# Opening of a conditioned decoder trunk: modulation blocks ahead of weight tiles in the load queue, and constant tiles multiplied on TensorE between the first transposes

## The chip, the cores and the metric

The kernel runs on one core of a Trainium2 chip. A core has TensorE (PE in the profile; its weight loads are shown apart as PEld), VectorE (DVE), ScalarE (ACT), GpSimd (POOL) and SyncE (SP), and 16 DMA engines that they share. The metric is the device time of one execution in microseconds; before the change the median of three runs is 1215.93 us (1215.64 to 1216.92).

## The reference

One decoder layer on `x` of 1024 tokens by 1024 channels, all in 32-bit floats, conditioned by one vector `c`. Two mixers, HGRN2 and GLA, run on the same normalised input, both fed by one wide projection `w_in`; each branch is projected back, merged by sigmoid gates, and one output projection and a final norm follow. The change is in the part that makes the conditioned input and its first products:

```python
c_act = jax.nn.silu(c)
mod = c_act @ ada_w[l] + ada_b[l]
shift, scale, gate = jnp.split(mod, 3, axis=-1)
h = rms_norm(x, norm_w[l]) * (1.0 + scale[:, None, :]) + shift[:, None, :]
proj = h @ w_in[l]
```

`ada_w` is 1024 by 3072, so shift and scale alone need 8 MB of weights, for one row of result.

## The kernel before, in words

Everything is laid out with channels on the 128 partitions: `h` transposed is eight tiles of 128 channels (index `d`, 0 to 7) by 1024 tokens, worked on in two halves of 512 tokens. Matrix products keep 32-bit accuracy by splitting each operand into a high part in a reduced 32-bit format and the rest (`split`: a cast on ScalarE, L196, then a subtraction on VectorE, L197) and adding three products: high by high, high by low, low by high (`products(d, (0, 1, 2))`, six output tiles each, L352).

The opening, up to about 67 us, computes six columns of tiles (the GLA queries and two of its keys, `NG = 6`) for the first 512 tokens, while everything arrives from memory:

- The first four row tiles of `x` are loaded, squared (L203), scaled by their inverse root mean square (L210) and turned by TensorE transposes (`turn_x`, L219: four transposes per `d`, one per row tile); `copy_x` (L224) takes the result out of PSUM.
- Shift and scale come in five blocks, `blocks`, of one or two channel tiles each: d = 0; 1 and 2; 3 and 4; 5 and 6; 7. `load_mod` (L251) loads one: four loads of 256 KB for a block of one tile, eight for a block of two. Half of the sum over the input channels is accumulated on VectorE (`add_mod`, L265 and L267), the other half on TensorE (`mm_mod`, L277); `end_mod` adds the two (L283), reduces over partitions with a matmul by ones (L287) and leaves the factors `modv` and `amul` (L290, L292).
- `make_h(0, d)` applies them (L233) and splits the result.
- The raw weights come as eight tiles of 128 rows by 768 columns, 384 KB each (`load_wg`, L315); `prep_wg` splits each. Tiles 0, 1, 2, 5, 6 and 7 use three places in a fixed buffer in turn, so tile 5 needs tile 0 to be split, tile 6 tile 1 and tile 7 tile 2.

In this part the order of the instructions on TensorE, ScalarE and VectorE is the order in which the code writes them (`tc.manual_schedule`, until `order.close()`). An engine works its instructions in that order, so one that waits holds up all behind it. All these loads go through the SP queue, in order too. GpSimd stores finished pairs of `h` tiles (`store_h`, L238) as they come. After the opening a planner orders the instructions by its own costs, and the rest of the kernel follows: attention, further products, the branch and output projections.

The order of the opening is, in short: the loads of block 0, weight tiles 0, 1, 2, block 1, tiles 3 and 4, block 2; then the norm of `x`; `transpose_x(0, x_t, 0)`; block 0's modulation; `prep_wg(0)`; and a loop over the blocks that for each makes its `h` tiles, prepares the weight tiles of the next block, accumulates the next block on VectorE, and puts the products of this block on TensorE with the next block's `mm_mod` and `end_mod` between them.

Of the kernel before, what the change touches and what calls it, by code (L numbers as in the profile page):

```python
# [9 lines left out]
F32 = mybir.dt.float32  # L10
# [73 lines left out]
def hybrid_trunk_kernel(  # L84
# [6 lines left out]
    nc = tc.nc  # L91
# [99 lines left out]
    def split(src, hi=None, lo=None):  # L191

        if hi is None:
            hi = S.get(list(src.shape[1:]), F32R)
            lo = S.get(list(src.shape[1:]), F32R)
        nc.scalar.copy(hi, src)  # L196
        nc.vector.tensor_sub(lo, src, hi.bitcast(F32))  # L197
        return hi, lo
# [12 lines left out]

    turned = {}

    def turn_x(half, xs, d):
        if d % 2 == 0:
            hT[half, d // 2] = S.get([2, 512])
        turned[half, d] = mtile()
        for i in range(4):
            nc.tensor.transpose(turned[half, d][:, i * P:(i + 1) * P], xs[i][:, d * P:(d + 1) * P], ident)  # L219
        if d == KT - 1:  # L220
            S.free(*xs)

    def copy_x(half, d):
        nc.scalar.copy(hT[half, d // 2][:, d % 2, :], turned.pop((half, d)))  # L224

    def transpose_x(half, xs, d):
        turn_x(half, xs, d)
        copy_x(half, d)
# [14 lines left out]
    def load_mod(bi):  # L243
        d0, nd = blocks[bi]
        kq = 4 // nd
        mods[bi] = []
        for kk in range(KT // kq):
            b = S.get([kq, 2, nd * P])
            for half in range(2):
                c0 = half * D + d0 * P  # L250
                nc.sync.dma_start(b[:, :, half, :], ada_w[0, kk * kq * P:(kk + 1) * kq * P, c0:c0 + nd * P].rearrange(  # L251
                    "(k p) f -> p k f", p=P))
            mods[bi].append(b)
# [17 lines left out]
    def mm_mod(bi):  # L271
        kq = 4 // blocks[bi][1]
        w = 2 * blocks[bi][1] * P
        mod_ps[bi] = mtile()
        for j in range(4):
            k = 4 + j
            nc.tensor.matmul(mod_ps[bi][32 * j:32 * j + 32, 0:w], cs32[:, k, :],  # L277
                             mods[bi][k // kq][:, k % kq].rearrange("p a f -> p (a f)"), start=True, stop=True)
# [29 lines left out]
    raws = {}  # L308

    def load_wg(k):  # L310
        if k in (3, 4):
            raws[k] = S.get([T])
        else:
            raws[k] = xb_f[:, (k % 5 % 3) * 768:(k % 5 % 3) * 768 + 768]
        nc.sync.dma_start(raws[k][:, 0:NG * P], w_in[0, k * P:(k + 1) * P, C_GQ:C_GQ + NG * P])  # L315

    def prep_wg(k):
        raw = raws.pop(k)
        split(raw[:, 0:512], wa_hi[k // 2][:, k % 2, :], wa_lo[k // 2][:, k % 2, :])
        split(raw[:, 512:768], wb_hi[k // 4][:, k % 4, :], wb_lo[k // 4][:, k % 4, :])  # L320
        if k in (3, 4):
            S.free(raw)

    g_state = {}
    wga = cp.tile([P, KT, 16], F32, name="wga")
# [33 lines left out]

    load_mod(0)  # L360
    load_wg(0)
    load_wg(1)
    load_wg(2)
    load_mod(1)
    load_wg(3)
    load_wg(4)
    load_mod(2)
    for i in range(4):
        square_x(i, x_t[i])
        scale_x(i, x_t[i])  # L370
    vec_rows(rows_a, 24, R_SH)
    transpose_x(0, x_t, 0)
    add_mod(0)
    mm_mod(0)
    end_mod(0)
    prep_wg(0)
    x_t2 = []
    for bi, (d0, nd) in enumerate(blocks):
        ds = range(d0, d0 + nd)
        more = bi + 1 < len(blocks)  # L380
        nxt = range(blocks[bi + 1][0], sum(blocks[bi + 1])) if more else ()
        for d in ds:
            make_h(0, d)
            if (0, d + 2) in turned:
                copy_x(0, d + 2)
        if not more:
            break
        for d in nxt:
            prep_wg(d)
        add_mod(bi + 1)  # L390
        if nd == 1:
            for d in nxt:
                transpose_x(0, x_t, d)
            products(d0, (0,))
# [1324 lines left out]
```

## Time and profile before

| | us |
|---|---|
| median of three runs | 1215.93 |
| the profiled execution | 1216.46 |
| its span (first to last instruction) | 1214.8 |
| TensorE busy in the span | 1184.1 |
| VectorE busy | 790.9 |
| ScalarE busy | 546.9 |

The page's row of 40 slices gives the shape: TensorE is busy 5 tenths of the first slice of 30 us and 9 tenths or more of every other but the last. The DMA engines are busy 9 and 8 tenths of the first two slices; later they are less than half busy in most slices.

How to read it: times in the views are from the start of the span. In a timeline row stand the start, the length, engine, line and operation, what it writes and reads with its shape, and how many of a kind were merged; in brackets how long the engine was idle before, and what ended the wait. A matmul's length includes the time to run through the array, so that matmuls of a row overlap: the step from one start to the next tells the rate. The busy time of TensorE is a union of such stretches. A 32-bit matmul that is not split stands as two passes.

### The profile page before, as it was taken

To read this page: it belongs to the slowest core of one execution; us is meant where nothing else is said; L and a number is where in the kernel's file an instruction comes from. 1 tells how busy PE (TensorE), PEld (TensorE's weight loads), DVE (VectorE), ACT (ScalarE), POOL (GpSimd) and SP (SyncE) were. 2 spreads that over 40 slices of the span, in tenths; PEclk is the share of its full clock that TensorE was granted. 3 is DMA by queue.
4 is the path that set the end of the run, shared out by engine and by line. 5 is a ranking of instruction groups with operands and counts; after the bars stand their busy time and mean duration, and the time that the engine had idled before them with its cause. 6 is when DMAs were issued, how large, how long until landed. Compare 5 with 4: busy or idle time off the path is not lost.

```text
span 1214.8 us, 20860 instructions
## 1 busy us (share of the span) xinstructions
PE 1184.1 (97%) x8579; PEld 982.6 (81%) x8579; DVE 790.9 (65%) x1245; ACT 546.9 (45%) x797; POOL 123.8 (10%) x215
## 2 busy tenths in 40 slices
PE   5999999999999999999999999999999999999997
PEld 3777889889798888888887888877778888878886
DVE  4637444774848456877884365794653775988994
ACT  5646732434434244344332324455743544444554
POOL 4100000202111121121110101011220000000000
PEclk9999999999999999999999999999999999999999
DMA  9814000844444267255341112054697746435523
GB/s 320 277 70 139 18 19 19 293 141 161 156 152 149 66 207 249 94 179 169 108 174 47 59 53 70 36 174 158 227 343 277 260 160 208 135 104 173 174 104 122
DMA packets 130961, 183.51 MB, mean 151 GB/s; under 512 B 7467, under 2 KB 97633, under 8 KB 130866
## 3 DMA queue, kind: packets, MB, share of 16 engines
q1 hardware_dynamic: 117250, 136.87, 35.7%
q0 software_dynamic: 13568, 45.31, 9.6%
q8 instruction: 67, 1.10, 0.4%
q14 instruction: 28, 0.23, 0.1%
q10 hardware_dynamic: 48, 0.01, 0.0%
HBM read 132.87 MB, written 49.28 MB: 150 GB/s over the span
## 4 chain that ended last, share of the span: by engine, by line
PE 61%; issue 23%; DVE 3%; ACT 3%; POOL 2%; DMA 1%; POOLq 0%; ACTq 0%; DVEq 0%
PE pd L541 19%; PE pd L1343 9%; PE sc_ps L1343 5%; PE pm L1343 5%; PE pd L1520 3%; PE pd L643 2%; PE pd L644 2%; PE pd L645 2%; PE sc_ps L1520 2%; PE pm L848 1%; PE pd L352 1%; PE pm L829 1%; PE pm L850 1%; PE pm L1520 1%; PE sc_ps L352 1%
## 5 line engine op out<-in xcount | busy, mean ns | idle before, releaser
L541 PE MATMUL pd<-b,b 128*128 128x512 f32 x1632 | 387.4, 394 | 0.0
L541 PEld LDWEIGHTS pd<-b,b 128*128 128x128 f32 x1632 | 302.4, 188 | 64.8 <-issue 1.4
L1343 PE MATMUL pd<-b,b 128*128 128x512 f32 x720 | 173.7, 392 | 4.3 <-ACT b L1414 2.1
L1343 PEld LDWEIGHTS pd<-b,b 128*128 128x128 f32 x720 | 133.7, 188 | 35.7 <-ACT b L1414 3.2
L197 DVE TENSOR_TENSOR b<-b,b 128x1024 fp32r<-128x1024 f32 (+2 forms) x89 | 98.9, 1122 | 83.1 <-ACT b L196 65.4
L196 ACT CAST b<-b 128x1024 fp32r<-128x1024 f32 (+2 forms) x89 | 82.9, 948 | 92.1 <-DVE b L1199 14.6
L1286 DVE TENSOR_TENSOR b<-b,b 128x1024 fp32r<-128x1024 f32 x56 | 68.3, 1224 | 66.9 <-ACT b L1285 52.3
L1285 ACT CAST b<-b 128x1024 fp32r<-128x1024 f32 x56 | 58.3, 1050 | 73.9 <-PE pd L1343 20.6
L1343 PE MATMUL sc_ps<-b,b 128*128 128x512 f32 x324 | 79.4, 391 | 1.0 <-ACT scT L793 1.0
L600 PE MATMUL pd<-b,b 128*128 128x256 f32 x256 | 74.2, 290 | 0.0
L1264 DVE TENSOR_TENSOR b<-b,b 128x1024 fp32r<-128x1024 f32 x48 | 59.2, 1251 | 20.8 <-ACT b L1263 15.1
L602 PE MATMUL pd<-b,b 128*128 128x256 f32 x256 | 72.5, 283 | 0.0
L601 PE MATMUL pd<-b,b 128*128 128x256 f32 x256 | 72.4, 283 | 0.0
L1343 PEld LDWEIGHTS sc_ps<-b,b 128*128 128x128 f32 x324 | 60.3, 188 | 14.6 <-ACT scT L793 1.4
L1343 PE MATMUL pm<-b,b 128*128 128x512 f32 x300 | 72.1, 389 | 0.0
L1263 ACT CAST b<-b 128x1024 fp32r<-128x1024 f32 x48 | 49.9, 1050 | 41.2 <-PE pd L1343 16.0
L1343 PEld LDWEIGHTS pm<-b,b 128*128 128x128 f32 x300 | 56.3, 188 | 11.7
L352 PE MATMUL pd<-b,b 128*128 128x512 f32 x192 | 53.3, 410 | 2.0 <-ACT b L196 0.9
L1201 POOL DMA_DIRECT2D ws<-b x64 | 34.6, 541 | 192.0 <-DVE b L1195 86.5
L735 ACT COPY xb<-b 128x512 f32<-128x512 f32 x48 | 29.4, 620 | 49.4 <-PE sc_ps L715 26.7
L643 PE MATMUL pd<-b,b 128*128 128x512 f32 x128 | 51.3, 401 | 0.0
L644 PE MATMUL pd<-b,b 128*128 128x512 f32 x128 | 50.0, 390 | 0.0
(285 smaller groups left out, 1964.3 us busy)
## 6 DMA issues: line engine op xcount, KB each, us to landing
b<-in_w_in_dram SPq DMA_DIRECT2D x66, 512.0 KB, 4.2
ws<-b POOLq DMA_DIRECT2D x64, 256.0 KB, 3.3
b<-ws SPq DMA_DIRECT2D x32, 512.0 KB, 4.9
b<-in_x_dram SPq DMA_DIRECT2D x16, 512.0 KB, 5.7
b<-in_ada_w_dram SPq DMA_DIRECT2D x32, 256.0 KB, 6.9
b<-in_w_branch_dram SPq DMA_DIRECT2D x16, 512.0 KB, 4.4
b<-h SPq DMA_DIRECT2D x14, 512.0 KB, 4.3
wo<-b POOLq DMA_DIRECT2D x14, 512.0 KB, 5.7
```

Of the source, the lines that this page charges most:

```text
L196: nc.scalar.copy(hi, src)
L197: nc.vector.tensor_sub(lo, src, hi.bitcast(F32))
L352: nc.tensor.matmul(accs[f], wg(a, d, f), b[d][:, half * 512:half * 512 + 512], start=(d == 0 and n == 0), stop=(d == KT - 1 and n == 2))
L541: nc.tensor.matmul(ps[0:w, th * 512:(th + 1) * 512], a[:, k, 0:w], b[:, th * 512:(th + 1) * 512], start=(k == 0 and n == 0), stop=(k == KT ...
L600: nc.tensor.matmul(o, lh, hi[:, k % 4, :], start=(k == 0), stop=False)
L601: nc.tensor.matmul(o, lh, lo[:, k % 4, :], start=False, stop=False)
L602: nc.tensor.matmul(o, ll, hi[:, k % 4, :], start=False, stop=(k == KT - 1))
L643: nc.tensor.matmul(o, lh, hi[:, k % 2, :], start=(k == 0), stop=False)
L644: nc.tensor.matmul(o, lh, lo[:, k % 2, :], start=False, stop=False)
L1286: nc.vector.tensor_sub(lo, t, hi.bitcast(F32))
L1343: nc.tensor.matmul(o, a[:, sl], c, start=(p in (1, 5) and kt == 0 and n == 0), stop=(kt == 3 and n == 2), skip_group_check=True)
L1520: nc.tensor.matmul(o, a, b, start=(p in (1, 5) and kt == 0 and n == 0), stop=(kt == 3 and n == 2), skip_group_check=True)
```

## The change

What it does, in five parts:

1. In the SP queue the second modulation block goes ahead of weight tiles 1 and 2, and the third ahead of tiles 3 and 4.
2. `keep_busy(n)` multiplies two constant tiles, `ones` and `ident`, `n` times on TensorE into columns of `sc_ps` that the first products overwrite later. Six calls stand before the first transpose, 4, 8, 4 and 3 behind the four transposes of `d = 0`, one behind `mm_mod(0)` and two ahead of the first products. The results are not used.
3. The splitting of weight tiles 1 and 2 leaves its place ahead of the second block's accumulation. The casts of tile 1 go behind the first `end_mod` in the loop; the subtractions of tile 1, and tile 2 whole, go between `make_h(0, 1)` and `make_h(0, 2)`.
4. `prep_wg` becomes `prep_hi` (both casts) and `prep_lo` (both subtractions); the work is the same.
5. The loads of tiles 6 and 7 and of the last two modulation blocks are written behind that splitting, since they reuse its buffers. Tile 5 stays where it was.

```diff
+    def keep_busy(n):
+        for _ in range(n):
+            nc.tensor.matmul(sc_ps[:, 512:640], ones, ident, start=True, stop=True)
+
+    def turn_x(half, xs, d, gaps=(0, 0, 0, 0)):
...
             nc.tensor.transpose(turned[half, d][:, i * P:(i + 1) * P], xs[i][:, d * P:(d + 1) * P], ident)
+            keep_busy(gaps[i])
...
+    def wg_parts(k):
+        return ((raws[k][:, 0:512], wa_hi[k // 2][:, k % 2, :], wa_lo[k // 2][:, k % 2, :]),
+                (raws[k][:, 512:768], wb_hi[k // 4][:, k % 4, :], wb_lo[k // 4][:, k % 4, :]))
+
+    def prep_hi(k):
+        for raw, hi, _ in wg_parts(k):
+            nc.scalar.copy(hi, raw)
+
+    def prep_lo(k):
+        for raw, hi, lo in wg_parts(k):
+            nc.vector.tensor_sub(lo, raw, hi.bitcast(F32))
         raw = raws.pop(k)
...
     load_mod(0)
     load_wg(0)
+    load_mod(1)
     load_wg(1)
     load_wg(2)
-    load_mod(1)
+    load_mod(2)
     load_wg(3)
     load_wg(4)
-    load_mod(2)
...
-    transpose_x(0, x_t, 0)
+    keep_busy(6)
+    turn_x(0, x_t, 0, (4, 8, 4, 3))
+    copy_x(0, 0)
     add_mod(0)
     mm_mod(0)
+    keep_busy(1)
     end_mod(0)
...
+            if bi == 1 and d == 1:
+                prep_lo(1)
+                prep_wg(2)
+                load_wg(6)
+                load_mod(3)
+                load_wg(7)
+                load_mod(4)
...
-        for d in nxt:
-            prep_wg(d)
+        if bi:
+            for d in nxt:
+                prep_wg(d)
         add_mod(bi + 1)
         if nd == 1:
             for d in nxt:
                 transpose_x(0, x_t, d)
+            keep_busy(2)
             products(d0, (0,))
             mm_mod(bi + 1)
             products(d0, (1,))
             end_mod(bi + 1)
+            prep_hi(1)
             products(d0, (2,))
...
             load_wg(5)
-            load_wg(6)
-            load_mod(3)
-            load_wg(7)
-            load_mod(4)
```

More of the change, by code (lines that the diff above doesn't have):

```diff
@@ L212, in hybrid_trunk_kernel @@
     turned = {}
-    def turn_x(half, xs, d):
+    def keep_busy(n):
+        for _ in range(n):
+            nc.tensor.matmul(sc_ps[:, 512:640], ones, ident, start=True, stop=True)
+    def turn_x(half, xs, d, gaps=(0, 0, 0, 0)):
         if d % 2 == 0:
@@ L315, in load_wg, with prep_wg @@
         nc.sync.dma_start(raws[k][:, 0:NG * P], w_in[0, k * P:(k + 1) * P, C_GQ:C_GQ + NG * P])
-    def prep_wg(k):
+    def wg_parts(k):
[7 more added lines that the diff above has]
+            nc.vector.tensor_sub(lo, raw, hi.bitcast(F32))
         raw = raws.pop(k)
-        split(raw[:, 0:512], wa_hi[k // 2][:, k % 2, :], wa_lo[k // 2][:, k % 2, :])
-        split(raw[:, 512:768], wb_hi[k // 4][:, k % 4, :], wb_lo[k // 4][:, k % 4, :])
         if k in (3, 4):
             S.free(raw)
+    def prep_wg(k):
+        prep_hi(k)
+        prep_lo(k)
     g_state = {}
```

## The prediction

> **What bounds the kernel now.** I read the page's head first, then busy time by stretches, then the timeline of the first 40 us engine by engine (TensorE, VectorE and ScalarE, the SP queue), and last the issue-to-landing times of single loads.
>
> ```profile
> span 1214.8 us, 20860 instructions
> ```
>
> ```profile
> 14.00:22.00 8.00, 6.71 (x26) 4.47 (x26) 5.48 (x13) 5.19 (x11) 1.30 (x5) 1.00 1.08 362
> 22.00:26.00 4.00, 3.61 (x17) 1.59 (x16) 3.05 (x5) 0.00 (x0) 0.00 (x0) 1.00 1.07 369
> 26.00:38.00 12.00, 11.13 (x63) 8.10 (x62) 6.92 (x13) 5.60 (x10) 0.59 (x1) 1.00 1.08 367
> 38.00:67.00 29.00, 29.00 (x153) 22.94 (x153) 16.71 (x36) 18.89 (x35) 6.11 (x9) 1.00 0.61 209
> 74.00:110.00 36.00, 35.19 (x165) 26.63 (x164) 14.66 (x28) 20.73 (x28) 1.59 (x3) 1.00 0.41 135
> 110.00:800.00 690.00, 688.64 (x6122) 586.53 (x6121) 437.72 (x780) 273.87 (x401) 79.61 (x111) 1.00 0.37 119
> 800.00:900.00 100.00, 95.17 (x658) 76.56 (x657) 66.81 (x89) 58.72 (x84) 16.71 (x27) 1.00 0.64 223
> 900.00:1207.00 307.00, 306.40 (x1346) 251.43 (x1344) 227.16 (x260) 147.60 (x202) 4.27 (x8) 1.00 0.53 177
> ```
>
> The columns after the stretch are its length, then busy time of PE, PEld, DVE, ACT and POOL, the granted clock, the DMA share and GB/s. The reader is to see three things. TensorE has no idle time at all from 38 to 67 us, and 0.81 + 1.36 + 4.83 + 0.60 = 7.6 us of it from 74 us to its end: whatever the opening gains or loses by 38 us is carried to the end nearly one for one. Until 38 us the 16 DMA engines are full (share over 1) at 362 to 369 GB/s: the opening is a queue of loads with work hung on it. And the clock column says 1.00 even where, in the next rows, the same matmul takes nearly twice as long.
>
> ```profile
> 7.34 0.48 PE L219 MATMUL pm<-ident,b 128*128 128x128 f32 x1 [3.99 <-DVE b L210]
> 13.11 0.47 PE L219 MATMUL pm<-ident,b 128*128 128x128 f32 x1 [1.21 <-DVE b L210]
> 14.47 1.08 PE L277 MATMUL pm<-b,cs 128*32 128x256 f32 x8 [0.88 <-DVE scT L267]
> 17.02 1.95 PE L219 MATMUL pm<-ident,b 128*128 128x128 f32 x8
> 19.17 2.07 PE L352 MATMUL pd<-b,b 128*128 128x512 f32 x4 [0.20 <-ACT b L196]
> 21.04 1.05 PE L352 MATMUL sc_ps<-b,b 128*128 128x512 f32 x2
> 23.47 1.05 PE L277 MATMUL pm<-b,cs 128*32 128x512 f32 x4 [0.39 <-DMA b<-in_ada_w_dram]
> 24.45 1.21 PE L352 MATMUL pd<-b,b 128*128 128x512 f32 x4
> 25.50 0.62 PE L352 MATMUL sc_ps<-b,b 128*128 128x512 f32 x2
> 28.92 1.20 PE L352 MATMUL pd<-b,b 128*128 128x512 f32 x4
> 35.72 0.62 PE L352 MATMUL sc_ps<-b,b 128*128 128x512 f32 x2
> 37.13 1.02 PE L287 MATMUL pm<-ones,scT 128*128 128x1 f32 x8 [0.79 <-DVE scT L283]
> ```
>
> Two product matmuls take 1.05 us at 21.0 and 0.62 us at 25.5: TensorE runs at about half speed until some point between 21.5 and 24.5 us. The wait at 23.47 is for the last load of the second modulation block (mod1). The wait at 37.13 is the last one before the solid stretch: the third block's reduction (L287) waits for its accumulation on VectorE. That instruction is my clock: what it does, the kernel does.
>
> ```profile
> 27.40 0.82 ACT L233 ACTIVATE b<-b,modv,amul 128x512 f32<-128x512 f32 x1 [5.67 <-DVE amul L292]
> 30.21 2.28 ACT L196 CAST b<-b 128x512 fp32r<-128x512 f32 x5
> 30.86 2.57 DVE L197 TENSOR_TENSOR b<-b,b 128x512 fp32r<-128x512 f32 x5 [1.27 <-ACT b L196]
> 33.34 0.48 DVE L265 TENSOR_SCALAR scT<-b,cs 128x512 f32<-128x512 f32 x1
> 33.86 2.33 DVE L267 SCALAR_TENSOR_TENSOR scT<-b,cs,scT 128x512 f32<-128x512 f32 x3
> ```
>
> VectorE runs without a break from 30.86: the low part of h(2), the low parts of weight tiles 3 and 4 (five L197), then the accumulation (L265, three L267), one sum with TensorE's half of the block (L283), and at 37.13 the reduction. From the start of L265 to the reduction is 37.13 - 33.34 = 3.79 us.
>
> ```profile
> 8.24 3.11 SPq L315 DMA_DIRECT2D xb<-in_w_in_dram  x3
> 11.40 6.31 SPq L251 DMA_DIRECT2D b<-in_ada_w_dram  x8
> 18.10 1.09 SPq L315 DMA_DIRECT2D b<-in_w_in_dram  x2
> 19.60 6.14 SPq L251 DMA_DIRECT2D b<-in_ada_w_dram  x8
> 26.19 1.08 SPq L315 DMA_DIRECT2D xb<-in_w_in_dram  x2
> ```
>
> ```profile
> b<-in_ada_w_dram SPq DMA_DIRECT2D x32, 256.0 KB, 6.9
> xb<-in_w_in_dram SPq DMA_DIRECT2D x6, 384.0 KB, 6.2
> ...
> h<-b POOLq DMA_DIRECT2D x8, 512.0 KB, 3.1
> ```
>
> The first view is the SP queue in order of time, the second the size of one load of each kind (L251 loads modulation blocks, L315 weight tiles) and of the store of h.
>
> **The change, part by part.** *Loads.* Per queue order now: weight tiles 0 to 2 (x3), mod1 (x8), tiles 3 and 4 (x2), mod2 (x8), tiles 5 and 6. New: tile 0, mod1, tiles 1 and 2, mod2, tiles 3 and 4, tile 5. So mod1 passes two tiles of 384 KB, 786 KB at 367 GB/s = 2.1 us: complete at 23.4 - 2.1 = 21.3. Tiles 1 and 2 fall behind mod1, to 22.3 and 23.4. Tiles 3 and 4 fall behind mod2. The set of bytes up to tile 4 is what it was up to the end of mod2, so tile 4 lands when the last mod2 load lands now:
>
> ```profile
> L251 SPq DMA_DIRECT2D b<-in_ada_w_dram x1: 368/368/368, 25.4 to 25.4; - x1
> ...
> DMA to landing us min/median/max: 5.9/5.9/5.9
> ```
>
> 25.4 + 5.9 = 31.3 us, where today it is issued near 18.9, ahead of mod2.
>
> *Constant tiles.* 28 calls of keep_busy (6 + 19 + 1 + 2). A 32-bit matmul here is two passes (four L277 calls stand as x8 in the rows), and a half-speed pass of 128 columns costs what a transpose does: (1.95 - 0.42)/7 = 0.22 us, so 0.43 us a call, half that at full speed. The first six (2.6 us) lie in the idle 3.99 us before 7.34. The 19 between the four transposes are 8.2 us at half speed from 7.34 and so push the fourth transpose from 13.11 to about 14.7 and mm_mod(0) from 14.47 to 16.3, unless the clock rises in between. In before, full speed came 7 to 10 us after the first dense work (14.47); the same span from 7.34 gives 14.4 to 17.3. At 14.4, which I take because the whole stretch is dense, mm_mod(0) starts at 15.4, its eight passes (1.08 us) and the four of the reduction each take half, 0.5 us less, and products(0) start about where they do today, at 19.1; at 17.3 they start 1.3 us later. Both are covered by the next wait: six product matmuls take 1.5 us at full speed (24.45 to 25.50 for four), and mm_mod(1) cannot finish before mod1 is in at 21.3 (with 17.3 it loses 0.5 us, which the wait for tile 4 below takes up).
>
> *First to second block.* mm_mod(1)'s last passes go from 23.47 to 21.4, and what hangs on them in one chain (L283, reduction, amul, L233 at 27.40, casts) moves by as much, 2.0 us: L233 at 25.4, the products of d=1 at 26.9 instead of 28.92. VectorE's accumulation, now ahead of the low parts of tiles 1 and 2, is done in time (it starts near 18.9 and takes 0.48 + 2.33 us).
>
> *Second to third block, where it is lost.* Between h(1) and h(2) ACT now also has tile 2's two casts (0.9 us: five casts with two tiles take 2.28) and VectorE the low parts of tiles 1 and 2 (1.9 us: h(2)'s and two tiles' take 33.34 - 30.86 = 2.48, of which h(2) 0.6). h(2)'s low part thus starts at 30.86 - 2.0 + 0.9 = 29.7. Then VectorE, in order, must do tiles 3 and 4 before add_mod(2), and tile 4 is only in at 31.3: cast 0.62, both low parts 0.9, with hand-overs L265 at 32.9 instead of 33.34, so 0.44 us earlier. TensorE's work there took from 28.92 to 36.34 = 7.4 us, starts at 26.9 and is through at 34.3; it stands idle for some 2.7 us, where it stood 0.79. The gained 2 us become a wait for a weight tile.
>
> *Store of h.* The first one follows L233 of d=1, so it is issued 2 us earlier than now, at 26.5.
>
> ```profile
> L238 POOL DMA_DIRECT2D h<-b x1: 586/586/586, 28.5 to 28.5; - x1
> ...
> DMA to landing us min/median/max: 6.5/6.5/6.5
> ```
>
> Its 524 KB are 1.4 us of DMA. If they go ahead of tile 4, L265 is 1.4 us later; if behind, nothing. With the same 6.5 us it lands at 33.0, behind tile 4: I stay near the lower end and take 0.3.
>
> *Moved loads.* On SP, tile 6 and mod3 now stand behind VectorE's low part of tile 1 (28.3 us instead of 26.9). The queue then still holds tiles 3 to 5 and the store, work until some 33.5 us, so the engines do not run dry; uncovered, the whole later queue would slip by up to 1.4 us, and the block that uses mod3 comes a whole block of products later.
>
> *Sum.* -0.44 + 0.3 = about -0.2 us at the reduction, and with TensorE solid after it, at the end. The profiled execution took 1216.46 us (span 1214.8 plus 1.7 around it), 0.5 over the median 1215.93; the difference is applied to the median: **1215.7 us**. Its own bounds: tile 4 early after all, then VectorE's order binds (29.7 + 2.48 = 32.2, -1.2): 1214.7; store ahead of tile 4, -0.44 + 1.4: 1216.9.
>
> **Rivals.** 0.2% (2.4 us) is about what a measurement of this kernel can tell from no change.
>
> *A: the clock falls back in the new idle stretch.* For it: 2.7 us idle is longer than any the trace has at full speed. Against: after the longest there, 1.82 us, nine matmuls run at full speed.
>
> ```profile
> 892.87 2.34 PE L1343 MATMUL pd<-b,b 128*128 128x512 f32 x9 [1.82 <-ACT b L1414]
> ```
>
> Price: half speed for as long as in the opening, at least 7.1 us (14.47 to 21.5), loses 3.5 us of solid work: 1219.2, slower. It decides if the fall sets in anywhere between 1.82 and 2.7 us of idle time; chance 0.11. The Trainium skill ("TensorE: Matmul & The Clock Gate", section "HAM oscillation — how this bites in real kernels") lets the clock fall when an idle gap crosses a window of about 3.4 us; by that rule 2.7 us is safe, the sum stays at 1215.7 and A would get no chance, and the trace, whose gaps end at 1.82 us, neither shows nor denies it.
>
> *B: the constant tiles do not raise the clock.* For it: one operand is mostly zeros, and the eight transposes at 17.02, back to back, did not raise it. Against: these are ordinary matmuls. Then mm_mod(0) starts 1.8 us late and the one call behind it adds 0.2: products(0) start at 21.1, need 2.6 us at half speed, and mm_mod(1) comes at 23.7, 2.3 us after mod1; its passes, the next six products and the reduction add some 2 us at half speed; 0.6 us of slack before tile 4 and the sum's 0.2 come off. +3.5 us, 1219.4; chance 0.05. The Trainium skill ("TensorE: Matmul & The Clock Gate", section "Part 4: PE-mode transpose") says that transposes do not count as busy for the clock as matmuls do; the eight at 17.02 agree, and by that rule the constant tiles count, the sum stays and B would get no chance.
>
> *C: the order after the hand-written part changes.* There the planner orders by its own costs, and it sees other times. The 7.6 us of idle time after 74 us are single waits of up to 1.82 us; two such more or less are 3.6 us: 1219.5 or 1212.3. Since 4.83 of the 7.6 lie in one stretch, 800 to 900 us, a new order there has more to win than to lose: 0.15 for faster, 0.08 for slower.
>
> *D: the 2.0 us carry through.* That needs add_mod(2) ahead of tiles 3 and 4 on VectorE, or a load queue that runs otherwise than I read it; the first the order forbids. 1213.9, which is still within 0.2%; chance 0.05.
>
> **How the numbers follow.** Forecast 0.56 and D 0.05: within 0.2% 0.61. A 0.11, B 0.05, C 0.08: slower 0.24. C: faster 0.15. The predicted time is the forecast's. The range reaches down to 1213.0, which leaves out C's better part (0.12), and up to 1219.3, just past A, which leaves out about half of B and C (0.07).
>
> **What would show it.** Right: product matmuls near 19 us at 0.39 us each; mm_mod(1) ending near 22.4; L233 of d=1 near 25.4; VectorE waiting for a cast that waits for a weight load near 31; a PE wait of some 2.7 us before the third block's L287 near 37.0. Wrong: that L287 before 36 or after 38; 0.63 us matmuls behind it (A) or near 20 us (B); new waits after 74 us (C).

## The result, and the profile after

The changed kernel is slower: 1223.84 us median (1222.82 to 1225.49, 6 runs) against 1215.93 (1215.64 to 1217.28) on the same chip, a ratio of 1.0064 with a 95% interval of 1.0051 to 1.0077, so +7.9 us. The forecast was 1215.7, and its range ended at 1219.3. The profiled execution took 1223.68 us.

Below are the head of the page of the changed kernel and its stretches (length, then busy time of PE, PEld, DVE, ACT and POOL, granted clock, DMA share, GB/s).

```profile
span 1222.0 us, 20967 instructions
...
26.00:38.00 12.00, 9.14 (x42) 5.56 (x40) 7.73 (x14) 5.94 (x12) 0.59 (x1) 0.98 1.07 375
38.00:67.00 29.00, 27.82 (x135) 22.15 (x136) 17.07 (x37) 16.47 (x31) 6.11 (x9) 0.89 0.61 198
...
110.00:800.00 690.00, 686.57 (x6097) 583.47 (x6096) 434.27 (x775) 275.92 (x401) 77.64 (x109) 1.00 0.36 118
```

Three things differ from before. In 26 to 38 us TensorE is busy for 9.14 us instead of 11.13. From 38 to 67 us, which was solid, it is idle for 1.2 us (the end of a wait that began at 35 us), and its granted clock is 0.89 instead of 1.00. And from 110 to 800 us it has 3.4 us of idle time instead of 1.4, in a part of the kernel that the change does not touch.

The opening on TensorE, and what feeds it on ScalarE and VectorE (start, length, operation; in brackets the idle time before it and what ended it). L282, L292 and L369 are what L277, L287 and L352 were before; L328 and L332 split weight tiles; L270 and L272 are the accumulation; L223 are transposes.

```profile
11.59 0.27 PE L223 MATMUL pm<-ident,b 128*128 128x128 f32 x1
...
18.35 1.21 PE L369 MATMUL pd<-b,b 128*128 128x512 f32 x4 [0.63 <-ACT b L196]
...
21.49 1.05 PE L282 MATMUL pm<-b,cs 128*32 128x512 f32 x4 [0.39 <-DMA b<-in_ada_w_dram]
...
39.18 1.84 PE L292 MATMUL pm<-ones,scT 128*128 128x1 f32 x8 [3.95 <-DVE scT L288]
40.88 2.05 PE L369 MATMUL pd<-b,b 128*128 128x512 f32 x4
```

```profile
25.41 0.82 ACT L238 ACTIVATE b<-b,modv,amul 128x512 f32<-128x512 f32 x1 [2.10 <-DVE amul L297]
...
32.08 0.93 ACT L328 CAST b<-b 128x512 fp32r<-128x512 f32 x2 [2.41 <-DMA b<-in_w_in_dram]
33.80 0.93 ACT L328 CAST b<-b 128x512 fp32r<-128x512 f32 x2 [0.79 <-DMA b<-in_w_in_dram]
```

```profile
29.70 0.69 DVE L197 TENSOR_TENSOR b<-b,b 128x512 fp32r<-128x512 f32 x1 [0.22 <-ACT b L196]
...
35.40 0.48 DVE L270 TENSOR_SCALAR scT<-b,cs 128x512 f32<-128x512 f32 x1
```

Up to 30 us the prediction holds step by step. Then weight tile 4 lands at 33.8 us instead of 31.3, the accumulation starts at 35.40 instead of 32.9, TensorE stands idle for 3.95 us instead of 2.7, and behind it everything runs at half speed until about 43.5 us: the eight passes of the reduction take 1.84 us (1.02 before), the next four product passes 2.05 instead of 1.2. That is rival A. The later course can be followed on matching instructions. First three of the changed kernel, then two of the kernel before; two more of that stand in the prediction or in a later fence (892.87, 313.46):

```profile
112.95 0.50 PE L369 MATMUL pd<-b,b 128*128 128x512 f32 x1 [0.66 <-DVE b L348]
...
866.24 0.50 PE L1369 MATMUL pd<-b,b 128*128 128x512 f32 x1 [0.99 <-ACT b L1341]
...
899.89 0.50 PE L1369 MATMUL pd<-b,b 128*128 128x512 f32 x1 [1.74 <-ACT b L1440]
```

```profile
108.68 0.50 PE L352 MATMUL pd<-b,b 128*128 128x512 f32 x1 [0.81 <-DVE b L331]
...
859.83 0.50 PE L1343 MATMUL pd<-b,b 128*128 128x512 f32 x1 [0.15 <-ACT b L1315]
```

At 109 us the changed kernel is 4.3 us late: 2.05 from the late reduction (39.18 against 37.13), the rest from the slow clock. At 860 us it is 6.4 late and at 893 it is 7.0. So 2.7 us come from later waits, although every engine has the same instructions in the same order behind the opening. That was in no step of the prediction, and the experiments had to find it.

### The profile page after: what moved, and what is told of

Same layout as the page of the kernel before. It is cut to its first block, busy times and chain, and to the rows that moved or that the text cites. A ratio compares the mean times of both kernels' runs of the same rounds, so it can differ in the third digit from the quotient of the medians.

```text
span 1222.0 us, 20967 instructions
## 1 busy us (share of the span) xinstructions
PE 1193.7 (98%) x8635; PEld 991.2 (81%) x8635; DVE 790.4 (65%) x1245; ACT 547.4 (45%) x797; POOL 124.2 (10%) x215
## 4 chain that ended last, share of the span: by engine, by line
PE 62%; issue 22%; DVE 3%; ACT 3%; POOL 2%; DMA 1%; POOLq 0%; ACTq 0%; DVEq 0%
PE pd L567 20%; PE pd L1369 9%; PE sc_ps L1369 5%; PE pm L1369 5%; PE pd L1546 3%; PE pd L669 2%; PE pd L671 2%; PE pd L670 2%; PE sc_ps L1546 2%; PE pm L874 1%; PE pd L369 1%; PE pm L876 1%; PE pm L855 1%; PE pm L1546 1%; PE sc_ps L709 1%
## 5 line engine op out<-in xcount | busy, mean ns | idle before, releaser
L1369 PEld LDWEIGHTS pd<-b,b 128*128 128x128 f32 x720 | 133.6, 188 | 37.4 <-ACT b L1440 3.1
L197 DVE TENSOR_TENSOR b<-b,b 128x1024 fp32r<-128x1024 f32 (+1 forms) x85 | 97.2, 1151 | 86.3 <-ACT b L196 66.6
L196 ACT CAST b<-b 128x1024 fp32r<-128x1024 f32 (+1 forms) x85 | 81.3, 969 | 94.7 <-DMA b<-in_w_in_dram 14.5
L369 PE MATMUL pd<-b,b 128*128 128x512 f32 x192 | 53.6, 412 | 2.3 <-ACT b L196 1.3
```

What stands on the lines that cost most here:

```text
L369: nc.tensor.matmul(accs[f], wg(a, d, f), b[d][:, half * 512:half * 512 + 512], start=(d == 0 and n == 0), stop=(d == KT - 1 and n == 2))
L1369: nc.tensor.matmul(o, a[:, sl], c, start=(p in (1, 5) and kt == 0 and n == 0), stop=(kt == 3 and n == 2), skip_group_check=True)
```

## The experiments

Each kernel ran beside the kernel before on one chip. The table has the ratio to it with its 95% interval, and the difference worked out from the ratio at 1216 us. A profile is one execution, and runs of one kernel differ by 2 to 10 us, so a trace shows a mechanism and the ratio shows the size.

| kernel | ratio (95%) | us |
|---|---|---|
| changed kernel | 1.0064 (1.0051 to 1.0077) | +7.8 |
| the same, again (h4) | 1.0069 (1.0048 to 1.0091) | +8.4 |
| e1: without constant tiles | 1.0008 (0.9998 to 1.0019) | +1.0 |
| e2: constant tiles alone | 1.0040 (1.0027 to 1.0053) | +4.9 |
| e3: changed, accumulation first | 1.0019 (1.0008 to 1.0030) | +2.3 |
| e4: changed, wait filled | 1.0036 (1.0024 to 1.0048) | +4.4 |
| g1: length alone | 1.0019 (1.0010 to 1.0028) | +2.3 |
| g2: changed, whole packet | 1.0016 (1.0004 to 1.0027) | +1.9 |
| g3: e3, whole packet | 0.9986 (0.9977 to 0.9995) | -1.7 |
| g4: e3 without constant tiles | 0.9984 (0.9973 to 0.9994) | -1.9 |
| h1: e4, whole packet | 1.0014 (1.0005 to 1.0023) | +1.7 |
| h2: e2, whole packet | 1.0003 (0.9994 to 1.0012) | +0.4 |
| h3: e2, sum of head 7 on VectorE | 1.0033 (1.0019 to 1.0047) | +4.0 |
| k1: e2, sum of head 6 on VectorE | 1.0048 (1.0034 to 1.0061) | +5.8 |
| k2: meant to store h later | 1.0051 (1.0039 to 1.0064) | +6.2 |
| k3: g4, sum of head 6 on VectorE | 0.9996 (0.9985 to 1.0006) | -0.5 |

### Either part alone, and the two links of the chain

**e1**, load order and splitting without constant tiles:

```diff
-    keep_busy(6)
-    turn_x(0, x_t, 0, (4, 8, 4, 3))
-    copy_x(0, 0)
+    transpose_x(0, x_t, 0)
...
-    keep_busy(1)
...
-            keep_busy(2)
```

> The changed kernel without its constant tiles (no keep_busy); load order and splitting as changed. My theory: 56 fewer passes on TensorE put the packets that fetch instructions back to about 36 us, the third block's loads land in one go, tile 4 lands near 32.5 us instead of 33.8 (the early store of h still goes ahead of it), the third block's reduction (L292 of the changed kernel) comes near 38.0 instead of 39.2, TensorE's idle time before it falls under 3 us and the clock stays full behind it; TensorE at 45 us stands +0.5 to +1.5 us to the kernel before instead of +4.3; time 1216.5 to 1218.5. Rival 1, the order of loads alone does it: tile 4 at 33.8, idle 3 to 4 us, clock falls, +4 us at 45 us, time 1220 to 1224. Rival 2, without the tiles the clock rises 7 us later and the opening loses that in front: mm_mod(1) ends 2 us later than in the changed kernel (23.5 instead of 21.5).

**e2**, the kernel before with the 28 calls of `keep_busy` at their places and nothing else.

> The kernel before with the constant tiles alone (28 calls of keep_busy at the same places); loads and splitting as before. My theory: mm_mod(1) still waits for its load at 23.4 us, so the earlier clock wins nothing; the fetch of instructions comes near 26 us as in the changed kernel and holds up loads in flight by up to 1.2 us, so the third block's reduction (L287 of before at 37.1) comes at 37.1 to 38.3; time 1215.9 to 1217.5. Rival, the longer TensorE program shifts the fetches of the whole kernel and with them the waits after 220 us: +2.8 us behind the opening here too, time 1218 to 1220.

**e3**, the changed kernel with the third block's accumulation ahead of tiles 3 and 4 on VectorE:

```diff
-        if bi:
+        if bi > 1:
             for d in nxt:
                 prep_wg(d)
         add_mod(bi + 1)
+        if bi == 1:
+            prep_wg(3)
+            prep_hi(4)
...
             end_mod(bi + 1)
+            if bi == 1:
+                prep_lo(4)
```

> The changed kernel with the third block's accumulation (add_mod(2)) ahead of weight tiles 3 and 4 on VectorE, and tile 4's low part behind end_mod(2). My theory: the reduction no longer waits for tile 4; it comes at 35.2 to 35.8 us when TensorE is through with its products, instead of 39.2, TensorE stands idle there under 1 us and the clock stays full: at 45 us TensorE is 1.5 to 2 us ahead of the kernel before, 6 us ahead of the changed one; time 1214 if nothing is added behind the opening, 1217 if the 2.8 us there come all the same. Rival, tile 4 is not what the block waits for (its own late load is, or the products of d=3 then wait for tile 3 and 4 just as long): a wait of 2 us or more remains between 35 and 42 us, time 1219 or more.

**e4**, the wait filled with products that nobody reads:

```diff
         pm = mtile()
+        if bi == 2:
+            for _ in range(14):
+                nc.tensor.matmul(pm[:, 256:384], ones, ident, start=True, stop=True)
```

> The changed kernel with 14 more constant products (28 passes, 3.1 us at full clock) on TensorE ahead of the third block's reduction, into columns of its own accumulator that nobody reads: the wait for tile 4 stays, the idle time goes. My theory: the reduction still comes at 39.2 us, but its passes and the products behind it run at 0.39 us for two passes instead of 1.05: TensorE at 45 us stands +2.0 us to the kernel before instead of +4.3; time 1221.5, 2.3 under the changed kernel. Rival, the clock does not fall through idleness (something else holds it, such as the loads): half-rate products between 39 and 43 us all the same, time 1223.8.

The reduction of the third block on TensorE's timeline, in e1, then in e3 and e4:

```profile
36.97 1.02 PE L287 MATMUL pm<-ones,scT 128*128 128x1 f32 x8 [1.60 <-DVE scT L283]
```

```profile
34.73 1.04 PE L292 MATMUL pm<-ones,scT 128*128 128x1 f32 x8 [0.45 <-ACT b L229]
```

```profile
34.17 3.29 PE L292 MATMUL pm<-ident,ones 128*128 128x128 f32 x28
37.33 1.05 PE L295 MATMUL pm<-ones,scT 128*128 128x1 f32 x8
```

e1 has the reduction at 36.97, where the prediction had 37.0 and e1's own expectation 38.0, a clock that holds, and a time that cannot be told from before. Its wait is only 1.60 us, because without the tiles TensorE's own work ends later (35.4 us instead of 34.4 in g2 below), so e1 does not test what a wait of 2.7 us does. The new load order alone neither wins nor loses. e3 shows that tile 4 is what the block waits for: with the accumulation ahead of it the reduction comes at 34.73, 2.4 us ahead of before. In e4 the clock holds; but its tile 4 was early too, so this run does not price the fall by itself.

The misses are in the totals. e2 should have cost nothing and costs 4.9 us, with an opening that is not late. e3 is 2.4 us ahead in the opening and ends 2.3 us behind. The constant tiles cost some 4 us far from where they stand.

### Why the tiles cost: the packets that carry instructions

The page's DMA part has queues of their own for instructions. The larger one stands alike in both kernels (a second, q14, has 28 packets and 0.23 MB in both):

```profile
q8 instruction: 67, 1.10, 0.4%
```

67 packets, 1.10 MB: 16 KB each. TensorE has 2 x 8635 matmul and load instructions in the changed kernel, 258 to a packet. The 28 calls add 112 instructions, so every later packet comes nearly half a packet earlier: in e2 at 27, 48, 70 and 101 us, in the kernel before at 35, 59, 80 and 112. Here are the DMA queues of the changed kernel in 24 to 28 us, and of the kernel before in 34 to 38 us, where its first packet is (packets, MB, share of 16 engines):

```profile
q1 hardware_dynamic: 1355, 1.40, 107.9%
q8 instruction: 1, 0.02, 1.7%
```

```profile
q1 hardware_dynamic: 1421, 1.37, 103.5%
q8 instruction: 1, 0.02, 1.8%
```

1.7% of 16 engines over 4 us is 1.1 us of one engine. In 24 to 28 us the queue of loads is full and carries the third block and tiles 3 and 4. That the packet holds up the part of a load that shares its engine is an inference: no view here shows the engines one by one.

To test this, tiny products were added: as many instructions as the tiles have, or as many more as make up one packet of 256.

```diff
+    def pad(n):
+        for i in range(n):
+            nc.tensor.matmul(sc_ps[32 * (i % 4):32 * (i % 4) + 32, 512:513], ident[:, 0:32], one_t,
+                             start=True, stop=True)
...
     vec_rows(rows_a, 24, R_SH)
+    pad(28)
```

**g1** is the kernel before with `pad(28)`; **g2** the changed kernel with `pad(36)`; **g3** is e3 with `pad(36)`; **h2** is e2 with `pad(36)`. **g4** is e3 without constant tiles and without `pad`.

> The kernel before with 28 tiny products (128x32 by 128x1, one column each) on TensorE behind the transpose of rows_a, in its idle time before 7.34 us; nothing else. They lengthen TensorE's program by as many instructions as the constant tiles (28 calls, 112 instructions) but are too short to change the clock or the opening. My theory now: TensorE's instructions come in packets of 16384 bytes, one per about 256 instructions, each a single packet on one DMA engine that holds up the loads of that moment by about 1 us; 112 instructions more move every later packet 8 to 13 us ahead of the work, as in the run with the tiles alone (first one near 27 us instead of 35, one at 299 us in the burst of loads of 291 to 302 instead of 287), and with them the waits at 253 to 315, 812 and 860 us. Expected: the opening within 0.3 us of the kernel before at 45 us, packets as in the tiles-alone run, time 1219 to 1221.5. Rival: the cost of the tiles is their work or the earlier clock, not the length: time 1216 to 1217, packets unmoved.

> The changed kernel with 36 tiny products more (128x32 by 128x1) ahead of its constant tiles: 64 calls, 256 instructions, one packet of instructions in whole, so that all packets behind the opening fall where they fall in the kernel before. My theory: packets near 35, 59, 80, 111 us as in the kernel before; tile 4 lands at 31.2 to 32.0 us instead of 33.8, the third block's reduction comes at 36.7 to 37.7 us instead of 39.2, the idle time ahead of it is under 2.7 us; behind the opening no more than 1 us is added; time 1216 to 1218, as without the tiles. Rival 1, length is not it: 1221 to 1224. Rival 2, a packet that now falls into 5 to 15 us delays the loads of the opening: L282 of the first block later than 15 us, and 1 us of that stays.

> The kernel with the third block's accumulation ahead of weight tiles 3 and 4 (constant tiles and new load order kept), with the same 36 tiny products more, a whole packet of instructions in all. My theory: the opening is 2.4 us ahead of the kernel before at 37 us as in that kernel's own run, and now stays so: no 2.4 us wait at 812 us and no fall of the clock behind it; time 1213.5 to 1215, under both kernels. Rival, the 4.7 us that kernel lost behind the opening come from its being early, not from the packets: time 1217.5 to 1219.

> The kernel with the third block's accumulation ahead of weight tiles 3 and 4, without any constant tiles: new load order, program length as before. My theory: the clock rises near 21 us as in the run without tiles, the reduction no longer waits for tile 4 and comes at 34.8 to 35.6 us (before 37.1, with tiles 34.7); packets as in the kernel before; time 1214 to 1215.5. Rival, without the tiles the slow clock until 21 us is now on the path: reduction at 36 us or later, time 1216 or more; or the early opening itself breeds the later waits: 1217.5 to 1219.

> The kernel with the constant tiles alone (old load order), with 36 tiny products more, 256 instructions in all. My theory: its 4.4 us over the kernel before come from packets of instructions moved by 112 instructions, and go: packets near 35, 59, 80, 287 us again, waits at 314 and 863 us back under 0.7 and gone, time 1215.5 to 1217.5. Rival: the tiles cost by the earlier clock or their work, whatever the length: 1219.5 to 1222.

36 more products on TensorE make three kernels faster: the changed kernel goes from +7.8 to +1.9, e3 from +2.3 to -1.7, e2 from +4.9 to +0.4. And length alone, with an opening like that of before, costs 2.3 us (1.2 to 3.4). So the cost hangs on where the packets fall, and not on the work of the tiles. How the packets turn into lost time can be followed at one place in the trace. In 291 to 303 us a burst of loads ends with a block that VectorE waits for; it feeds the totals for which TensorE waits near 314 us. The queues and the row of VectorE in e2, then in g1:

```profile
q8 instruction: 1, 0.02, 0.6%
...
302.61 0.69 DVE L1204 TENSOR_TENSOR b<-b 128x512 f32<-128x512 f32 x1 [1.71 <-DMA b<-in_w_in_dram]
...
314.10 0.89 PE L724 MATMUL sc_ps<-xb,b 128*32 128x48 f32 x64 [1.40 <-DVE tot L727]
```

```profile
q8 instruction: 1, 0.02, 0.6%
...
303.04 0.69 DVE L1201 TENSOR_TENSOR b<-b 128x512 f32<-128x512 f32 x1 [1.62 <-DMA b<-in_w_in_dram]
...
314.52 0.89 PE L721 MATMUL sc_ps<-xb,b 128*32 128x48 f32 x64 [1.30 <-DVE tot L724]
```

The same rows of the kernel before and of h2, where no instruction packet falls into this stretch:

```profile
301.72 0.69 DVE L1195 TENSOR_TENSOR b<-b 128x512 f32<-128x512 f32 x1 [0.71 <-DMA b<-in_w_in_dram]
...
313.46 0.89 PE L715 MATMUL sc_ps<-xb,b 128*32 128x48 f32 x64 [0.66 <-DVE tot L718]
```

```profile
301.18 0.69 DVE L1210 TENSOR_TENSOR b<-b 128x512 f32<-128x512 f32 x1 [0.64 <-DMA b<-in_w_in_dram]
...
312.73 0.89 PE L730 MATMUL sc_ps<-xb,b 128*32 128x48 f32 x64 [0.40 <-DVE tot L733]
```

With a packet in the burst the block is in 0.9 to 1.9 us later and TensorE waits 1.3 to 1.4 us instead of 0.4 to 0.7. The Trainium skill ("Runtime: NRT & Kernel Launch", section "Instruction fetch mechanics") says that instructions come in 16 KiB blocks of 256 and that crossing a boundary costs little and is mostly hidden. The size agrees. It is hidden from TensorE in so far as no wait of it here ends on an instruction; it is not hidden from the loads.

The traces of the other kernels agree. Behind the opening TensorE works the same instructions in the same order in all of them, so that its delay against the kernel before can be read instruction by instruction. At this place, between 308 and 318 us, the delay grows by 0.6 to 1.0 us in all nine kernels whose packets are shifted (the changed kernel, h4, e2, e3, e4, g1, h3, k1, k2) and shrinks by 0.1 to 0.4 us in the seven others. From 862 to 895 us it grows by 0.4 to 1.3 us in eight of the nine (not in e4) and in none of the seven. A third loss, 0.5 to 1.4 us near 255 us, stands in all nine, but about 1 us of it also in e1, g3 and k3, so that the packets are not its only cause.

What length alone costs (2.3) is less than what a whole packet takes away (4.0 to 5.9). The profiled executions show where the rest lies. e2 and e3 lose 2.5 us near 813 us, by a wait with a fall of the clock behind it that g1 does not have (its cause is below). At 45 us the changed kernel is 1.6 us later than g2, because tile 4 comes late. Whether the shift brings about the loss near 813 us is not shown.

Constant tiles without the shift win nothing: g2 and e1 cannot be told apart, nor g3 and g4. **g4 has the lowest ratio, 1.9 us under before** (0.7 to 3.3), with no constant tiles at all. Its reduction:

```profile
35.03 1.04 PE L287 MATMUL pm<-ones,scT 128*128 128x1 f32 x8 [0.47 <-ACT b L224]
```

### Why the clock falls

g2 is the changed kernel with the packets where they were. ScalarE's casts of tile 4, VectorE's accumulation and TensorE's reduction in it, and its stretches:

```profile
31.39 0.93 ACT L333 CAST b<-b 128x512 fp32r<-128x512 f32 x2 [0.16 <-DMA b<-in_w_in_dram]
```

```profile
33.00 0.48 DVE L275 TENSOR_SCALAR scT<-b,cs 128x512 f32<-128x512 f32 x1
```

```profile
36.78 1.67 PE L297 MATMUL pm<-ones,scT 128*128 128x1 f32 x8 [2.42 <-DVE scT L293]
38.31 2.05 PE L374 MATMUL pd<-b,b 128*128 128x512 f32 x4
```

```profile
36.00:40.00 4.00, 3.22 (x12) 2.96 (x13) 0.96 (x3) 1.08 (x2) 0.00 (x1) 0.62 1.09 355
40.00:44.00 4.00, 4.00 (x11) 3.09 (x11) 2.95 (x6) 3.34 (x7) 0.54 (x1) 0.53 1.15 324
...
647.60:651.40 3.80, 3.80 (x11) 2.97 (x11) 1.23 (x1) 0.69 (x2) 0.00 (x0) 0.55 0.30 79
```

Tile 4 (31.4), accumulation (33.0) and reduction (36.8) are the forecast's 31.3, 32.9 and 37.0. The idle time is 2.42 us where 2.7 were forecast, and it is enough: the clock falls, and at 44 us TensorE is 2.9 us behind before, from 0.35 ahead.

**h1** fills that wait as e4 did, with `pad(22)` so that all calls together make a whole packet.

> The changed kernel with a whole packet of instructions in all (22 tiny products ahead of the constant tiles) and with 14 more constant products ahead of the third block's reduction, which fill the wait for tile 4 that was 2.42 us idle in the run with the whole packet alone. My theory: the clock no longer falls behind the reduction (it cost 2.8 us there), so TensorE at 45 us is within 0.6 us of the kernel before, against +2.6 to +2.8 in the run with the whole packet; time 1216 to 1217.5, 2 to 3 under that run's. Rival, the fall has another cause than the idle time: half-rate products behind 37 us and 1219 to 1220 as there.

```profile
38.18 0.95 PE L300 MATMUL pm<-ones,scT 128*128 128x1 f32 x8
```

The clock holds, although the reduction comes later than in g2, and at 109 us TensorE stands at +0.6 us instead of +2.6: the mechanism is as expected. The total is not: +1.7 against +1.9, where 2 to 3 us less were expected; 2 us is at the edge of what the two intervals allow, so the run does not bear the price out. This execution lost 1.6 us again near 648 us, by a fall of the clock such as g2 has at 647.6 (the row above). It follows four short products of norms that take 4.1 us (two passes each start about 1 us apart), without idle time. The kernel before has the same four and a clock of 1.00 behind them in its profiled execution; of all 17 profiled executions four show this fall (g2, h1, h4 and k1). So the clock falls in some executions and not in others, without a wait. In how many of the runs behind the ratios of g2 and h1 the clock fell, at 37 us or here, is not known.

### The changed kernel again, and three edits that settled less

**h4** is the changed kernel once more.

> The changed kernel once more, unchanged, beside the others on the same chip. My theory: tile 4 lands at 31.5 to 34 us, by which DMA engine the packet of instructions near 25 us hits (the run with the clock kept had 32.0 with the same packet), so the wait before the third block's reduction is 2.0 to 4.0 us, always long enough for the clock to fall; time 1220.5 to 1224. Rival: the 33.8 us is the rule: wait 3.9 us and 1223 to 1225 again.

```profile
39.17 1.06 PE L292 MATMUL pm<-ones,scT 128*128 128x1 f32 x8 [3.81 <-DVE scT L288]
40.10 2.06 PE L369 MATMUL pd<-b,b 128*128 128x512 f32 x4
```

Tile 4 came at 33.8 us again and the time is 1224.15 us, so the rival of this expectation holds. The clock falls again, here behind the reduction: the products take 2.06 us. **k2** was to store h later (`for i in (1, 0, 2, 3)` in `store_h`):

> The changed kernel with its first store of h (0.5 MB) behind the second: pieces in the order 1, 0, 2, 3, so that none is stored before 43 us. My theory: tile 4 landed at 33.8 us because one DMA engine, held up by the packet of instructions near 26 us, gets to tile 4's last pieces when the store (32 to 34 us) already shares it; without the store tile 4 lands at 32.0 to 32.8 us and the reduction comes at 37.4 to 38.2 instead of 39.2; the wait is still over 2 us and the clock still falls: 1222 to 1223, 1 to 1.5 under the changed kernel. Rival: the store has no part in it: 33.8 and 39.2 us as before, 1224.

The planner orders GpSimd's queue by when data are ready, and the first store was still issued at 25.5 us. So k2 is the changed kernel a third time, and the part of the store stays untested. In k2 tile 4 lands at 32.0 us, the wait is 3.37 us and the reduction comes at 37.4 us, so 33.8 us for tile 4 is not the rule either. Its load, in the changed kernel (8.2 us to land in k2), and in g2:

```profile
L320 SPq DMA_DIRECT2D b<-in_w_in_dram x1: 341/341/341, 24.9 to 24.9; - x1
...
DMA to landing us min/median/max: 8.9/8.9/8.9
```

```profile
L325 SPq DMA_DIRECT2D b<-in_w_in_dram x1: 340/340/340, 24.8 to 24.8; - x1
...
DMA to landing us min/median/max: 6.6/6.6/6.6
```

Without the packet among these loads tile 4 takes 6.6 us to land (6.4 in e1, 6.8 in h1), with it 8.9 and 8.2, but 6.8 in e3 and 7.2 in e4, which have the packet there too. In h1 a packet comes at 19 us, among the loads of tiles 1 and 2: these take 7.7 and 7.9 us, where g2's take 6.2 and 6.4. So a packet can cost more than its own 1.1 us or nearly nothing. Which loads' pieces it meets may decide that, and the store may add to it; neither was tested.

**h3** and **k1** are e2 with one sum of squares on VectorE instead of GpSimd (`(nc.vector if h == 7 else nc.gpsimd).tensor_add(...)`, in k1 `h == 6`); **k3** is g4 with that of k1. The reason was this meeting near 798 us, VectorE and GpSimd in e2, then VectorE in the kernel before:

```profile
798.59 3.09 DVE L694 TENSOR_TENSOR b<-b,b 128x256 f32<-128x256 f32 x1
...
798.77 2.40 POOL L1116 TENSOR_TENSOR b<-b,b 128x1024 f32<-128x1024 f32 x1
...
813.48 6.68 PE L1352 MATMUL pd<-b,b 128*128 128x512 f32 x21 [2.36 <-DVE b L962]
```

```profile
799.10 2.21 DVE L679 TENSOR_TENSOR xb<-xb,b 128x256 f32<-128x256 f32 x1
```

> The kernel with the constant tiles alone, its last sum of squares over the heads (one 128x1024 sum near 798 us) on VectorE instead of GpSimd. In the traces a 128x256 operation on VectorE that meets this sum takes 2.2 us in the kernel before and 3.1 us with the tiles, instead of 0.42 to 0.63, and TensorE then waits 1.49 or 2.36 us near 812, the second with a fall of the clock. My theory: without the GpSimd sum that stall goes, the wait near 813 us is under 1.6 us and the clock stays: 2 to 3 us under the tiles-alone run's 1220.9, 1218 to 1219; the waits at 314 and 863 us, from the packets, stay. Rival: the stall is none of GpSimd's, or comes back at the next one: wait of 2.3 us and 1220 to 1222.

> The kernel with the constant tiles alone, now with the sum of squares of head 6 on VectorE: that is the one near 798 us (the earlier attempt moved head 7's, near 852, and left this one on GpSimd); some splits behind it change places. My theory: the 128x256 operation that took 3.1 us there takes 0.7, the wait near 813 us is under 1.6 us in place of 2.36 and the clock does not fall behind it, 2.5 us under the tiles-alone run's 1220.9: 1218 to 1219, about what the length alone costs. Rival: the 2.36 us wait was that one profiled execution's; the rest of the cost lies elsewhere: 1220 to 1222.

> The kernel with the new load order, no constant tiles and the third block's accumulation ahead of weight tiles 3 and 4 (1214.9, 0.16% under the kernel before), with the sum of squares of head 6 on VectorE. My theory: the operation on VectorE that met the GpSimd sum near 796 us goes from 2.2 to under 1 us, the wait near 809 us from 1.48 to under 1.3 us; 1214.3 to 1215, 0.1 to 0.6 us gained. Rival: the sum itself (1.2 us on VectorE) takes the place of the stall and nothing is gained or 0.5 us lost: 1215 to 1215.5.

h3 moved the wrong head's sum, so the meeting is still there; but in its execution it stalls another operation of that shape, for 2.21 us as in the kernel before, and TensorE waits 1.43 us and not 2.36. In k1 the operation takes 0.66 us and the wait is 1.17 us, so the stall does come from GpSimd's sum. The traces of all kernels sort by it: in e2, e3 and e4 the operation takes 3.09 us, TensorE waits 2.36 to 2.38 us and the clock falls, 2.5 us in all; in every other one with this sum on GpSimd it takes 2.2 us, the wait is 1.4 to 1.5 us and the clock holds. Still, k1 costs 5.8 us, no less than e2's 4.9: its profiled execution lost 1.5 us by 45 us and 1.6 us near 648 us to other falls of the clock. So the meeting explains 2.5 us of e2's and e3's profiled executions, but taking it away did not make the kernel faster. k3 won nothing either.

k1's trace shows the first of these falls. With the tiles the first products are done early, and TensorE waits for the second modulation block. Its wait in k1 and the granted clock behind it, then the same wait in h2:

```profile
21.99 1.05 PE L282 MATMUL pm<-b,cs 128*32 128x512 f32 x4 [2.05 <-DMA b<-in_ada_w_dram]
...
24.00:26.00 2.00, 2.00 (x6) 0.59 (x3) 0.58 (x1) 0.00 (x0) 0.00 (x0) 0.50 1.09 350
```

```profile
21.91 1.05 PE L287 MATMUL pm<-b,cs 128*32 128x512 f32 x4 [1.96 <-DMA b<-in_ada_w_dram]
```

k1's clock fell at 2.05 us of idle time and TensorE lost some 1.5 us; h2's, at 1.96, did not, nor h3's at 1.99.

## Why the prediction was wrong, point by point

At 893 us the changed kernel is 7.0 us late: 2.05 us from the late reduction, 2.2 from the slow clock behind it (read at 109 us), 2.7 from later waits. The forecast had 0.2 us gained, no fall of the clock and nothing later. Two of its steps failed: the cost of the constant tiles, which it counted without their instructions, and the clock, which it kept up behind an idle time of 2.7 us. The first is behind the late tile 4 and most of the later waits; the second stands on its own, for in g2, with the packets in place, the clock fell too.

- **Loads.** mod1 complete at 21.3: its last passes wait until 21.49. Right.
- **Constant tiles raise the clock.** Right (rival B fell), and sooner than the 14.4 I took: the transpose at 11.59 takes 0.27 us. That gain is covered by mod1, as the step said: products at 18.35, forecast 19.1.
- **The cost of the 28 calls.** Here the prediction failed. The step counted their time on TensorE and left out that they are 112 instructions that must be fetched. That moves the packets of instructions against the loads and costs 4.0 to 5.9 us, the difference that 36 products more take away in three kernels; 2.3 us of such a cost are shown for length alone. The prediction reads the queues of SP and GpSimd and not the instruction queue, though the page has a row for it.
- **First to second block.** L233 at 25.4, products at 26.9, h(2)'s low part at 29.7: measured 25.41, 26.93 and 29.70. Right.
- **Second to third block.** Tile 4 at 31.3 and L265 at 32.9: right in g2 (31.4, 33.0), where the packets lie as before, and 2.5 us early for the changed kernel (33.8, 35.4). The term was right for loads without the packet; in the changed kernel the packet falls among them.
- **Store of h**, taken as 0.3 and bounded by 1.4. Issued at 26.5 as forecast. In g2 and e1 tile 4 was in on time and the store cost nothing. In the changed kernel its part is open.
- **The idle time of 2.7 us.** It was 2.42 in g2, and 3.95 in the changed kernel. The sum gave it no price: it had TensorE solid, at full speed, behind it. That failed in both.
- **Rival A** was the right mechanism with too small a chance: 0.11. Its point of decision, between 1.82 and 2.7 us, holds: the clock fell behind 2.42 us. Its price of 3.5 us was near: by 45 us 3.2 in g2 and 2.4 in the changed kernel. In part that is luck: it took the 7.1 us of the opening, and the granted clock was 0.50 for 6.8 us in these two, but for 3.4 us in h4. Forecast and A together made 1219.2, +3.3; g2, the change without its packets, has +1.9 (0.5 to 3.3). The Trainium skill ("TensorE: Matmul & The Clock Gate", section "HAM oscillation — how this bites in real kernels") was cited for a window of about 3.4 us, by which 2.7 us would be safe. The runs deny it as a safe limit: 2.42 and 2.36 us were enough. Another section of that page ("Part 1: The HAM clock gate (the "warmup" mystery)") says that the window runs freely; then how a wait lies in it decides, which would fit 2.05 falling and 1.96 not; no run tests it.
- **Rival C** named new waits after 74 us, but by a new order. The order behind the opening is the same on all engines, so C as put is false. The waits came with the packets, as far as the places at 314 and at 862 to 895 us show it, and C had 0.15 for faster where there was only a loss.
- **Rival D** was held impossible under the order as written, rightly. With the order changed (e3, g4) the reduction comes 2.1 to 2.4 us ahead of before: the 2.0 us were there to be had.
- **"Whatever the opening gains or loses is carried to the end"** holds only while nothing else moves: the changed kernel was 4.3 us late at 109 us and 7.0 at 893, and e2, on time in the opening, ended 4.9 late.

## What to carry to other kernels

Where the DMA queue is full, added instructions can cost more than their time: count them, look at where the instruction packets fall among the loads before and after, and test with a padding of one whole packet before the edit itself is blamed. A wait of 2 us or more on TensorE puts the clock at risk and should be priced with a fall (1.6 to 3.2 us here). A load that is moved ahead helps only if what is queued in front of its consumer is moved too: here the accumulation on VectorE was the edit that paid, and the constant tiles paid nothing.

## What the runs showed of the hardware

- An instruction packet is one transfer of 16 KB that takes 1.1 us of one DMA engine's time (1.7% of 16 engines over 4 us), about one for 256 TensorE instructions (258 by count). With one among full loads, the load of tile 4 (384 KB) took 6.8 to 9.0 us to land, and 6.4 to 6.8 without.
- TensorE's clock fell behind waits of 2.36 to 2.42 us and longer, once behind 2.05, and in four of 17 executions without any idle time, behind 4.1 us of short products; it held behind 1.82, 1.96 and 1.99. In g2 it also fell at 16.5 us, for 3.4 us, shortly after it had first risen and behind waits of only 1.12 and 0.21 us. The granted clock shows such falls (0.50 to 0.62 in the stretches above), while the slow start before 21 us in the kernel before stands there as 1.00.
- A 128x256 operation on VectorE took 2.2 to 3.1 us beside a 128x1024 sum on GpSimd, and 0.66 without. The Trainium skill ("Advanced Engine Details and Errata", section "VectorE Performance Modes") notes that VectorE's second port is shared with GpSimd, and that GpSimd instructions and VectorE instructions that use two ports block each other; the times agree, but no run shows whether this operation uses two.
